# Five edits to the order and size of ScalarE work in a float32 decoder layer

## The chip, the cores and the metric

The kernel runs on one core of one Trainium2 chip. The metric is the device time of one execution in microseconds (us). The core has these engines: TensorE (PE, matrix products), VectorE (DVE), ScalarE (ACT), GpSimd (POOL) and SyncE (SP, which here only starts weight transfers). Each engine works through its own queue of instructions in order; an instruction that has to wait holds up all that stand behind it on the same engine.

## The reference

One decoder layer with 256 tokens, 2048 channels, all in float32:

```python
h = rmsnorm(x, attn_norm_w)
z, xbc, dt_raw, q, k, v, g = split(h @ w_in)
y_ssm  = ssd_mixer(z, xbc, dt_raw, ...) @ w_ssm_out     # 8 groups of 8 heads of 64
y_attn = moba_attention(q, k, v, ...) @ w_attn_out      # 16 heads of 128
g_ssm, g_attn = split(sigmoid(g + b_gate))
x = x + (g_ssm * y_ssm + g_attn * y_attn) @ w_out
h = rmsnorm(x, ffn_norm_w)
u_gate, u_up = split(causal_dwconv(h @ w_up, ...))
x = x + (silu(u_gate) * u_up) @ w_down
```

Inside `ssd_mixer`, the columns `xbc` pass a causal convolution of four taps and silu; silu is also taken of `z`, which multiplies the mixer's result; each group is then normed by its root mean square. With 256 tokens there is one chunk and one attention block, so attention is plain causal attention with a bias by distance, after a norm of each head's query and key.

## The kernel before

**Products.** TensorE takes float32 data in a rounded form, so each operand is split into a high part (a rounded copy) and a low part (the rest), and a product is high x high + high x low + low x high. A weight is fetched in units of 128 x 2048 (1 MB, tile `wraw`, three buffers, started by SP). `unit` (L188) splits each unit in two chunks of 1024 columns: ACT copies the high part (`whi`, L198), DVE subtracts for the low part (`wlo`, L199), three buffers of each. `cm_chunk` (L227) then issues, for each k of a chunk, one matmul of 512 columns with the high part (L234), and afterwards one of 256 columns with the low part (L240). Where the accumulator is only 256 wide, the first becomes two (L237, L238). `last_hi` remembers the high part traced last, and `after_hi()` (L218) puts what is traced in its block behind that high part on ACT's queue: an order of issue, no wait.

**Order.** The Python code is traced once; a scheduler then orders each engine's queue. It issues what is ready first, and among ready instructions the one traced earlier. In the attention stage PE's order alone is fixed as traced. `issue_after(ins)` adds an edge of order.

**The steps of the work, in the order of the trace:**

- Values (L433): column blocks of 512, four units each (`tm_units`, L410; matmuls L401, L402, L407). While block 0 runs, x arrives. After block 1's first unit, `x_squares` (L339) squares x on ACT in four parts of 1024 columns and adds them on DVE (L343 to L345). After the first chunk of that block's third unit, `x_stats` (L347) sums over channels on PE (L350, L312) and forms the norms.
- Attention (`attn_pair`, L469), eight pairs of heads, four units each. What follows the units of a pair is cut into steps that a `Spread` runs one per unit ("tick"): sums of squares at tick 1, the norm at tick 3 (`norm`, L502, with multiplies on GpSimd, L517, for six of the eight pairs), the split of keys and queries at tick 5 (`split`, L519: ACT copies L523, DVE and GpSimd subtract, L525), scores at tick 6. Ahead of pair 6 stands the fourth value column.
- Gates of attention and the attention output.
- The mixer, nine steps. In step g, `group_units` (L779) makes the group's 10 units: four of z (into `pr[:, 0:4]`), then six that pass the convolution (into `pr[:, 4:10]`). Beside them run `core_steps` of the group before: `silu` (L801), transposes, decays (`dec`, L847, with Exp, L860), products (`ydot`, L870), the group's norm (L893 to L905, with Ln and Exp, L329 and L330). `silu` is one activation over all ten parts and is followed by an early load of the ACT table set that holds both Ln and Exp (L804). In steps 1 and 2 four units of the mixer's gates are made each and stored to DRAM (`gs`); in step 8 the other eight stay in `pre[0]`. Steps 3 to 8 also run units of the output product (`out_unit`, L924).
- The last quarter of the output product (L993): eight units, each followed by `merge` (L973). It multiplies the mixer's result by its gate, adds the stored attention part (`ma`) and splits the sum into `mt` (L990, L991). For units 0 to 3 the gate is fetched from `gs` on GpSimd's queue (L977), and two sigmoids follow (L980, L981): of that gate and of a pair of those in `pre[0]`. Both are held behind the last group's norm.
- `out_products` (L1006): the product with `w_out`. The first two units are run together: chunk 0 of both, then chunk 1 of both. x is fetched again for it from ACT's queue (L1002).
- The FFN: up, gate, down, in three thirds.

Of the kernel before, what the change touches and what calls it, by code (L numbers as in the profile page):

```python
# [8 lines left out]
F32 = mybir.dt.float32  # L9
F32R = mybir.dt.float32r  # L10
AF = mybir.ActivationFunctionType
ALU = mybir.AluOpType
AX = mybir.AxisListType
MUL, ADD, SUB, MAX, MIN = ALU.mult, ALU.add, ALU.subtract, ALU.max, ALU.min

DM, T, DI, G, NS, H, HD, DFF = 2048, 256, 4096, 8, 128, 16, 128, 5632
# [109 lines left out]
def mix(x):  # L126
    return x.rearrange("p (a b) -> p b a", a=2)


def mixed(ps):  # L130
    return ps.rearrange("p (b a) -> p b a", a=2)
# [40 lines left out]
def build(nc, d, out):  # L172
    with tile.TileContext(nc) as tc:
        _body(tc, nc, d, out)


def _body(tc, nc, d, out):
    V, S, PE = nc.vector, nc.scalar, nc.tensor
# [39 lines left out]
    def after_hi():  # L218
        return tc.issue_after(last_hi[0].ins) if last_hi[0] is not None else contextlib.nullcontext()

    def mm_tile():
        return psum.tile([128, 512], F32, name="mm", bufs=4)
# [4 lines left out]
    def cm_chunk(ps, part, x2, k0, nk, first, last):  # L227
        hi, lo = part
        wide = ps.shape[-1] == 2 * T
        for k in range(nk):  # L230
            w = hi[:, k * 128:(k + 1) * 128]
            start = first and k == 0
            if wide:
                PE.matmul(ps.rearrange("p (h b a) -> p h b a", h=2, a=2), w,  # L234
                          x2[:, :, k0 + k].rearrange("p h (a b) -> p h b a", a=2), start=start, stop=False)
            else:
                PE.matmul(mixed(ps), w, mix(x2[:, 0, k0 + k]), start=start, stop=False)  # L237
                PE.matmul(mixed(ps), w, mix(x2[:, 1, k0 + k]), start=False, stop=False)  # L238
        for k in range(nk):
            PE.matmul(mixed(ps[:, :T]), lo[:, k * 128:(k + 1) * 128], mix(x2[:, 0, k0 + k]), start=False,  # L240
                      stop=last and k == nk - 1)
# [23 lines left out]
    def r32(name):  # L265
        t = base.tile([128, 2, 16, T], F32R, name=name, tag="s32", bufs=3)
        return t, t[:, 0], t[:, 1]
# [4 lines left out]
    sq = xt_full[:, 16 * T:].rearrange("p (k t) -> p k t", t=T)  # L272
# [44 lines left out]
    def hp_split(k):  # L317
        x = xt[:, k] if k else x0[:, KT:KT + T]
        a = S.activation(hph[:, k], x, AF.Copy, scale=aw[:, k:k + 1])
        return a, V.scalar_tensor_tensor(hpl[:, k], x, aw[:, k:k + 1], hph[:, k].bitcast(F32), op0=MUL, op1=SUB)  # L320

    last_rsq = [None]
# [13 lines left out]
    rb = base.tile([128, T], F32, name="rb")  # L336
    base.tile([128, 16], F32, name="pad1")

    def x_squares():  # L339
        for c in range(4):  # L340
            S.activation(sq[:, 4 * c:4 * c + 4], xt[:, 4 * c:4 * c + 4], AF.Square)
        for c in range(1, 4):
            V.tensor_tensor(sq[:, 0:4], sq[:, 0:4], sq[:, 4 * c:4 * c + 4], op=ADD)  # L343
        V.tensor_tensor(sq[:, 0:2], sq[:, 0:2], sq[:, 2:4], op=ADD)
        V.tensor_tensor(sq[:, 0], sq[:, 0], sq[:, 1], op=ADD)  # L345

# [22 lines left out]
    def bias_rows():  # L369
        rel = ap.tile([REL_BUCKETS + 1, H], F32, name="rel")  # L370
        oh = ap.tile([REL_BUCKETS + 1, 384], F32, name="oh")
        nc.sync.dma_start(rel, d["rel"])
        nc.sync.dma_start(oh, d["onehot"])
        ap.tile([128, 16], F32, name="pad4c")
        ohr = ap.tile([REL_BUCKETS + 1, 384], F32R, name="ohr")
        rels = ap.tile([REL_BUCKETS + 1, 2, H], F32R, name="rels")
        V.tensor_copy(ohr, oh)
        S.activation(rels[:, 0], rel, AF.Copy)
        V.tensor_tensor(rels[:, 1], rel, rels[:, 0].bitcast(F32), op=SUB)
        pb = c_tile()  # L380
        PE.matmul(pb[:H, :384], rels[:, 0], ohr, start=True, stop=False)
        PE.matmul(pb[:H, :384], rels[:, 1], ohr, start=False, stop=True)
        rows = ap.tile([H, 384], F32, name="brows")
        V.tensor_copy(rows, pb[:H, :384])
        nc.gpsimd.dma_start(brow, rows)

    def qk_constants():
        V.tensor_scalar(kscale, sm("kn"), HD ** 0.5, None, op0=MUL)
        same = ap.tile([128, 32], F32, name="same")
        V.tensor_reduce(same, ident.rearrange("p (b i) -> p i b", i=32), axis=AX.X, op=ADD)  # L390
        V.tensor_copy(sel, same[:, None, :].to_broadcast([128, 4, 32]))
# [41 lines left out]
    for cb in range(3):  # L433
        def before(k):
            if k == 0:
                nc.sync.dma_start(xt[:, 1:3], d["xT"][:, 1:3])
            elif k % 2 == 1 and k < 15:
                nc.sync.dma_start(xt[:, k + 2:min(k + 4, 16)], d["xT"][:, k + 2:min(k + 4, 16)])
            elif k == 15:
                nc.sync.dma_start(xt[:, 0:1], d["xT"][:, 0:1])  # L440
            return hp_split(k)

        def after(u, cb=cb):
            if cb == 1 and u == 0:
                with after_hi():
                    x_squares()
            if cb == 1 and u == 2:
                nc.sync.dma_start(small, d["small"])
            if cb == 0 and u == 3:
                bias_rows()  # L450
            if cb == 2 and u == 0:
                qk_constants()
        pst = tm_units(d["wv"][cb], after, before if cb == 0 else None, (lambda: x_stats(ap)) if cb == 1 else None)
        if cb == 0:
            evac0 = pst
            continue
        if cb == 1:
            evac(0, evac0)
        evac(cb, pst)
# [9 lines left out]
    def attn_pair(j):  # L469
# [49 lines left out]
        def split():  # L519
            for key in "kq":  # L520
                n = st["n" + key]
                t = ap.tile([128, 2, 2, T], F32R, name=key + "hl", bufs=1)
                S.activation(t[:, 0], n, AF.Copy)  # L523
                E = V if key == "k" or j in (0, 7) else nc.gpsimd
                E.tensor_tensor(t[:, 1], n, t[:, 0].bitcast(F32), op=SUB)  # L525
                st[key] = t
# [99 lines left out]
    gs = [dram.tile([128, 2, T], F32, name=f"gs{i}") for i in range(KT // 4)]  # L626
# [27 lines left out]
    gate_pool = base  # L654
# [39 lines left out]
    for o in range(KT):  # L694
# [8 lines left out]
        g = gl.pop(o)  # L703
        t = xb.tile([128, T], F32, name="wat", bufs=2)
# [11 lines left out]
    sd = ssd.enter_context(tc.tile_pool(name="ssd", bufs=1))  # L716
# [6 lines left out]
    o = (KT + 10) * T  # L723
# [72 lines left out]
    def core_steps(g):  # L796
        pr = pre[g % 2]
# [1 line left out]
        steps = []  # L799

        def silu():  # L801
            last = S.activation(pr, pr, AF.Silu)
            with tc.issue_after(last.ins):
                S.preload_act_table_set(LN_EXP)  # L804
            bh = sd.tile([128, 2, T + 16], F32R, name="bch")[:, :, :T]
            bl = sd.tile([128, 2, T + 16], F32R, name="bcl")[:, :, :T]
            S.activation(bh, pr[:, 8:10], AF.Copy)
            V.tensor_tensor(bl, pr[:, 8:10], bh.bitcast(F32), op=SUB)
            st["b"] = (bh, bl)

            st["x"] = sd.tile([128, 2, 4, 4, 64], F32R, name="xx")
# [158 lines left out]

    mt2, mh_, ml_ = r32("mt")

    def merge(u, ps):  # L973
        os_ = slice(2 * u, 2 * u + 2)
        if u < 4:
            g = gate_pool.tile([128, 2, T], F32, name="g", bufs=3)
            nc.gpsimd.dma_start(g, gs[u])  # L977
            late = pre[0][:, 2 * u:2 * u + 2]
            with tc.issue_after(last_rsq[0].ins):
                S.activation(g, g, AF.Sigmoid)  # L980
                S.activation(late, late, AF.Sigmoid)  # L981
        else:
            g = pre[0][:, 2 * u - 8:2 * u - 6]
        a = gate_pool.tile([128, 2, T], F32, name="g", bufs=3)
        nc.gpsimd.dma_start(a, ma[u])
        y4 = yacc[:, os_].rearrange("p o (a b) -> p o a b", a=2)
        V.tensor_tensor(y4, ps, y4, op=ADD)
        V.tensor_tensor(yacc[:, os_], yacc[:, os_], g, op=MUL)
        V.tensor_tensor(a, yacc[:, os_], a, op=ADD)
        S.activation(mh_[:, os_], a, AF.Copy)  # L990
        V.tensor_tensor(ml_[:, os_], a, mh_[:, os_].bitcast(F32), op=SUB)  # L991
# [14 lines left out]
    def out_products():  # L1006
        parts = [unit(d["wout"][o]) for o in range(2)]
        pss = [mm_tile() for _ in range(2)]
        for c in range(2):
            for o in range(2):  # L1010
                cm_chunk(pss[o], parts[o][c], mt2, 8 * c, 8, c == 0, c == 1)
        for o in range(KT):
            yield o, pss[o] if o < 2 else cm_unit(d["wout"][o], mt2)

# [4 lines left out]
    for o, ps in out_products():  # L1019
# [6 lines left out]
        else:  # L1026
            t = fp.tile([128, T], F32, name="sqx", bufs=2)
# [91 lines left out]
```

## Time and profile before

| | |
|---|---|
| median of 3 runs | 1955.76 us (1955.42 to 1956.25) |
| the profiled execution | 1955.65 us |
| its span in the profile | 1953.9 us |
| PE busy | 1943.7 us, 99% |
| DVE busy | 1576.6 us, 81% |
| ACT busy | 1253.3 us, 64% |
| GpSimd busy | 78.5 us, 4% |
| granted TensorE clock | 1.00 |
| moved by DMA | 401.81 MB, mean 206 GB/s |

The span is the time from the first to the last instruction that the profiler recorded; the execution's own time is 1.75 us longer. Instructions are named by the line of the kernel that issued them, as "L198 ACT", with the tiles that they write and read. Work of a helper has the helper's line. A row of the timeline gives start, length, engine, line, operation, tiles, shape, count, and in brackets how long the engine had stood idle and who ended it. A row of windows gives the stretch, its width, and then each engine's busy time with its number of instructions: PE, weight loads (PEld), DVE, ACT, POOL; then the granted clock and the DMA's share and rate.

### The profile page before, as it was taken

What the parts mean: (1) busy time and instruction counts of PE and PEld (TensorE: products, weight loads), DVE (VectorE), ACT (ScalarE), POOL (GpSimd) and SP (SyncE); (2) the same over time, 40 slices, a digit from 0 to 9 for tenths busy, and PEclk for the clock granted to TensorE, in tenths of its full rate; (3) what the DMA queues carried; (4) which work ended last, traced back from release to release, by engine and by line L of the source; (5) the groups of instructions that cost most, each with busy time, mean ns of one, the idle gap of its engine ahead of it and who ended that gap; (6) DMA issues with size and microseconds to landing.
All of it is one profiled execution on the core that took longest, in us unless ns stands there. A gap on an engine that the chain in (4) does not pass through costs nothing.

```text
span 1953.9 us, 31462 instructions
## 1 busy us (share of the span) xinstructions
PE 1943.7 (99%) x12287; PEld 1791.6 (92%) x12287; DVE 1576.6 (81%) x2461; ACT 1253.3 (64%) x1894; POOL 78.5 (4%) x100
## 2 busy tenths in 40 slices
PE   9999999999999999999999999999999999999999
PEld 7899899999989999999999998999999999999998
DVE  7588878867789898898989977788888885788665
ACT  6567666545778778777777745566666654566433
POOL 0012210000000000000000000000000000000000
PEclk9999999999999999999999999999999999999999
DMA  8555555766556656555565676555555555555555
GB/s 300 196 198 173 180 192 200 259 210 219 189 192 236 216 183 215 200 208 187 201 217 185 211 267 213 197 207 200 195 206 202 195 206 203 195 204 205 194 191 175
DMA packets 64317, 401.81 MB, mean 206 GB/s; under 512 B 7655, under 2 KB 10264, under 8 KB 20648
## 3 DMA queue, kind: packets, MB, share of 16 engines
q1 hardware_dynamic: 55384, 376.56, 54.6%
q0 software_dynamic: 5760, 18.97, 3.2%
q10 hardware_dynamic: 3024, 4.27, 0.7%
q8 instruction: 96, 1.57, 0.3%
q14 instruction: 53, 0.43, 0.1%
HBM read 394.44 MB, written 5.33 MB: 205 GB/s over the span
## 4 chain that ended last, share of the span: by engine, by line
PE 91%; DVE 3%; ACT 3%; issue 2%; DMA 1%; POOL 1%; DVEq 0%; ACTq 0%; POOLq 0%
PE mm L234 51%; PE mm L240 29%; PE mm L237 3%; PE mm L238 3%; DVE wlo L199 2%; ACT whi L198 1%; PE mm L407 1%; PE mm L401 1%; PE mm L402 1%; PE cc L880 1%; POOL nq L517 0%; PE cc L881 0%; DMA wraw<-wv 0%; PE cc L829 0%; DMA g<-gs 0%
## 5 line engine op out<-in xcount | busy, mean ns | idle before, releaser
L198 ACT ACTIVATE whi<-wraw 128x1024 fp32r<-128x1024 f32 (+1 forms) x712 | 742.3, 1046 | 491.1 <-PE mm L234 349.1
L199 DVE TENSOR_TENSOR wlo<-wraw,whi 128x1024 fp32r<-128x1024 f32 (+1 forms) x712 | 862.2, 1217 | 231.7 <-ACT whi L198 227.6
L234 PE MATMUL mm<-hn,whi 128*128 128x512 f32 x1536 | 363.6, 380 | 1.0 <-ACT whi L198 1.0
L234 PE MATMUL mm<-fh,whi 128*128 128x512 f32 x1408 | 333.3, 379 | 0.1
L234 PEld LDWEIGHTS mm<-hn,whi 128*128 128x128 f32 x1536 | 276.1, 190 | 32.9 <-ACT whi L198 1.2
L234 PEld LDWEIGHTS mm<-fh,whi 128*128 128x128 f32 x1408 | 253.1, 190 | 28.7 <-DVE fh L1022 0.5
L240 PEld LDWEIGHTS mm<-hn,wlo 128*128 128x128 f32 x1536 | 201.4, 191 | 10.3
L240 PE MATMUL mm<-hn,wlo 128*128 128x256 f32 x1536 | 202.4, 275 | 0.0
L240 PEld LDWEIGHTS mm<-fh,wlo 128*128 128x128 f32 x1408 | 184.5, 191 | 9.4
L240 PE MATMUL mm<-fh,wlo 128*128 128x256 f32 x1408 | 185.5, 275 | 0.0
L234 PE MATMUL mm<-hp,whi 128*128 128x512 f32 x768 | 183.2, 381 | 0.9 <-ACT whi L198 0.8
L234 PE MATMUL mm<-a,whi 128*128 128x512 f32 x692 | 164.9, 379 | 0.0
L234 PEld LDWEIGHTS mm<-hp,whi 128*128 128x128 f32 x768 | 138.1, 190 | 17.3 <-ACT whi L198 1.7
L234 PEld LDWEIGHTS mm<-a,whi 128*128 128x128 f32 x692 | 123.8, 190 | 13.5
L237 PE MATMUL mm<-yt,whi 128*128 128x256 f32 x512 | 117.8, 275 | 1.1 <-ACT whi L198 1.1
L238 PE MATMUL mm<-yt,whi 128*128 128x256 f32 x512 | 117.7, 275 | 0.0
L240 PEld LDWEIGHTS mm<-hp,wlo 128*128 128x128 f32 x768 | 100.7, 191 | 5.1
L240 PE MATMUL mm<-hp,wlo 128*128 128x256 f32 x768 | 101.2, 275 | 0.0
L237 PEld LDWEIGHTS mm<-yt,whi 128*128 128x128 f32 x512 | 98.3, 192 | 1.6 <-ACT whi L198 1.5
L238 PEld LDWEIGHTS mm<-yt,whi 128*128 128x128 f32 x512 | 98.3, 192 | 0.3
L240 PEld LDWEIGHTS mm<-a,wlo 128*128 128x128 f32 x704 | 93.4, 191 | 5.0
L1017 DVE TENSOR_TENSOR x<-mm,x 128x256 f32<-128x256 f32 x126 | 53.0, 420 | 53.7 <-PE mm L240 53.7
(315 smaller groups left out, 2464.0 us busy)
## 6 DMA issues: line engine op xcount, KB each, us to landing
wraw<-wup SPq DMA_DIRECT2D x88, 1024.0 KB, 4.8
wraw<-wssd SPq DMA_DIRECT2D x80, 1024.0 KB, 4.8
wraw<-wqk SPq DMA_DIRECT2D x32, 1024.0 KB, 4.7
wraw<-wso SPq DMA_DIRECT2D x32, 1024.0 KB, 4.8
wraw<-wd SPq DMA_DIRECT2D x32, 1024.0 KB, 4.8
wraw<-wga SPq DMA_DIRECT2D x16, 1024.0 KB, 5.0
wraw<-wao SPq DMA_DIRECT2D x16, 1024.0 KB, 5.2
wraw<-wgs SPq DMA_DIRECT2D x16, 1024.0 KB, 4.8
```

Of the source, the lines that this page charges most:

```text
L198: last_hi[0] = S.activation(hi[:, :n // 2], raw[:, s], AF.Copy)
L199: V.tensor_tensor(lo[:, :n // 2], raw[:, s], hi[:, :n // 2].bitcast(F32), op=SUB)
L234: PE.matmul(ps.rearrange("p (h b a) -> p h b a", h=2, a=2), w, x2[:, :, k0 + k].rearrange("p h (a b) -> p h b a", a=2), start=start, stop= ...
L237: PE.matmul(mixed(ps), w, mix(x2[:, 0, k0 + k]), start=start, stop=False)
L238: PE.matmul(mixed(ps), w, mix(x2[:, 1, k0 + k]), start=False, stop=False)
L240: PE.matmul(mixed(ps[:, :T]), lo[:, k * 128:(k + 1) * 128], mix(x2[:, 0, k0 + k]), start=False, stop=last and k == nk - 1)
L401: PE.matmul(mixed(pst[tt]), hph[:, k0 + k, ts], mix(wh), start=first and k == 0, stop=False)
L402: PE.matmul(mixed(pst[tt]), hpl[:, k0 + k, ts], mix(wh), start=False, stop=False)
L407: PE.matmul(mixed(pst[tt]), hph[:, k0 + k, ts], mix(wl), start=False, stop=last and k == 1)
L880: PE.matmul(pt, x0, mt[:, 0:256], start=True, stop=False)
L1017: V.tensor_tensor(halves(x), unmix(ps[:, h * T:(h + 1) * T]), halves(x), op=ADD)
```

## The change

- `x_squares` takes a part: squares 0 and 1 (and one add) after block 1's first unit, squares 2 and 3 (and the other adds) after its second, each behind that unit's high parts.
- The ACT copy of keys and queries in `split` is put behind the high part traced last.
- `silu` becomes two activations: first the six convolved parts, then the four of z. The early table load stays behind the second.
- The four stored gates get one tile, `early`, in the place of tile `xx` of the mixer, and are fetched by four transfers ahead of all merges. The sigmoids are put behind the high part traced last, no longer behind the norm.
- The first two units of `out_products` run k 0 to 7, 8 to 13, 14 and 15, each for both units.

```diff
-    def x_squares():
-        for c in range(4):
+    def x_squares(part):
+        cs = range(2 * part, 2 * part + 2)
+        for c in cs:
             S.activation(sq[:, 4 * c:4 * c + 4], xt[:, 4 * c:4 * c + 4], AF.Square)
-        for c in range(1, 4):
-            V.tensor_tensor(sq[:, 0:4], sq[:, 0:4], sq[:, 4 * c:4 * c + 4], op=ADD)
+        for c in cs:
+            if c:
+                V.tensor_tensor(sq[:, 0:4], sq[:, 0:4], sq[:, 4 * c:4 * c + 4], op=ADD)
+        if part == 0:
+            return
...
-            if cb == 1 and u == 0:
+            if cb == 1 and u < 2:
                 with after_hi():
-                    x_squares()
+                    x_squares(u)
...
-                S.activation(t[:, 0], n, AF.Copy)
+                with after_hi():
+                    S.activation(t[:, 0], n, AF.Copy)
...
         def silu():
-            last = S.activation(pr, pr, AF.Silu)
+            S.activation(pr[:, 4:10], pr[:, 4:10], AF.Silu)
+            last = S.activation(pr[:, 0:4], pr[:, 0:4], AF.Silu)
             with tc.issue_after(last.ins):
                 S.preload_act_table_set(LN_EXP)
...
+    early = sd.tile([128, 4, 2, T], F32, name="early", tag="xx")
+    for u in range(4):
+        nc.gpsimd.dma_start(early[:, u], gs[u])
+
     def merge(u, ps):
...
         if u < 4:
-            g = gate_pool.tile([128, 2, T], F32, name="g", bufs=3)
-            nc.gpsimd.dma_start(g, gs[u])
+            g = early[:, u]
             late = pre[0][:, 2 * u:2 * u + 2]
-            with tc.issue_after(last_rsq[0].ins):
+            with after_hi():
                 S.activation(g, g, AF.Sigmoid)
                 S.activation(late, late, AF.Sigmoid)
...
-        for c in range(2):
+        for k0, nk in ((0, 8), (8, 6), (14, 2)):
             for o in range(2):
-                cm_chunk(pss[o], parts[o][c], mt2, 8 * c, 8, c == 0, c == 1)
+                part = [p[:, k0 % 8 * 128:] for p in parts[o][k0 // 8]]
+                cm_chunk(pss[o], part, mt2, k0, nk, k0 == 0, k0 == 14)
```

## The prediction

> **What bounds the kernel now.** I read the page first: busy time by engine.
>
> ```profile
> span 1953.9 us, 31462 instructions
> PE 1943.7 (99%) x12287; PEld 1791.6 (92%) x12287; DVE 1576.6 (81%) x2461; ACT 1253.3 (64%) x1894; POOL 78.5 (4%) x100
> ```
>
> TensorE (PE) is busy all but 10.2 us. The change removes no matmul, so it can only win PE's idle moments, or make new ones. The view of waits, for PE alone, has two large rows:
>
> ```profile
> PE mm L234 <- ACT whi L198: 1.9, 2, 1.0
> PE mm L237 <- ACT whi L198: 1.1, 2, 0.8
> ```
>
> PE waits above all for a weight's high part (L198), late on ScalarE (ACT). I then cut the span at all places where PE stands (width, then PE busy; the difference is idle):
>
> ```profile
> 34.00:37.00 3.00, 2.38 (x12) 1.77 (x11) 3.00 (x4) 1.06 (x1) 0.00 (x0) 1.00 0.52 202
> 211.00:213.00 2.00, 1.18 (x6) 0.71 (x5) 0.81 (x1) 2.00 (x4) 1.25 (x1) 1.00 0.01 4
> 522.50:524.50 2.00, 1.66 (x14) 1.38 (x13) 1.49 (x3) 2.00 (x5) 0.00 (x0) 1.00 0.00 0
> 579.00:581.00 2.00, 0.97 (x8) 0.75 (x7) 1.73 (x4) 1.98 (x4) 0.00 (x0) 1.00 0.93 381
> 1147.00:1148.50 1.50, 1.22 (x11) 1.03 (x10) 0.77 (x1) 1.50 (x3) 0.00 (x0) 1.00 0.00 0
> 1155.00:1157.50 2.50, 1.66 (x15) 1.47 (x14) 1.57 (x3) 2.50 (x4) 0.54 (x1) 1.00 0.81 301
> 1179.00:1181.00 2.00, 1.39 (x7) 0.88 (x7) 2.00 (x3) 1.49 (x2) 0.00 (x0) 1.00 0.20 82
> ```
>
> Last, the chain of waits (start, length, engine and line), from which later parts draw too:
>
> ```profile
> 521.05 1.28 ACT L804
> ...
> 526.33 0.89 PE mm L240 x8
> 527.22 1.73 PE mm L234 x8
> ...
> 575.00 1.28 ACT L802
> 576.30 2.34 ACT pre L802
> ...
> 580.65 1.99 PE mm L234 x8
> ```
>
> Eight matmuls take 1.73 us in the flow and 1.99 behind a late high part. So a stall costs its idle time and 0.26 us: 0.88 at 34, 1.08 at 211, 0.60 at 522, 1.29 at 579, 0.54 at 1147, 1.10 at 1155, 0.87 at 1179.
>
> **The squares, halved.** On ACT, VectorE (DVE) and PE:
>
> ```profile
> 25.68 3.89 ACT L341 ACTIVATE xt<-xt 128x1024 f32<-128x1024 f32 x4
> 30.54 3.87 DVE L343 TENSOR_TENSOR xt<-xt 128x1024 f32<-128x1024 f32 x3
> 34.32 1.22 DVE L199 TENSOR_TENSOR wlo<-wraw,whi 128x1024 fp32r<-128x1024 f32 x1
> 37.19 0.41 DVE L345 TENSOR_TENSOR xt<-xt 128x256 f32<-128x256 f32 x1
> 41.74 0.50 PE L350 MATMUL cc<-ones,xt 128*128 128x1 f32 x4
> ```
>
> Three adds hold DVE, and the low part at 34.32 is what PE waits for. After: one add (3.87 / 3 = 1.29 us) stands ahead of it, and it is done 2.6 us sooner. Two squares (two times 0.97 us, on ACT), two adds and the short sums (L344, L345) follow one unit later; with the same work in all on DVE, and one low part more ahead of them, L345 ends near 37.6 + 1.2 = 38.8. PE reaches L350 at 41.74 - 0.88 = 40.9: 2.1 us of cover, in which the sum's split (ACT, then DVE) still has to pass. If that is gone, PE waits up to 0.5. Value: -0.88 (bounds -0.9 and 0).
>
> **The split of keys and queries: nothing.** I counted the high parts (L198) issued before the split of pair 4, which stalls PE at 211, and before that of pair 5:
>
> ```profile
> 0.00:208.05 208.05, 67.75 (x65) 1.00 0.62 215
> 0.00:230.72 230.72, 74.96 (x72) 1.00 0.61 211
> ```
>
> The split of a pair is traced at its fifth tick, so behind the next pair's last unit; for pair 4 that is pair 5. High parts up to there: 16 for two value columns and 6 pairs of 8, so the new edge names number 64, and 65 stand ahead already. For pair 5 (its fifth tick ends the fourth value column, 8 more) it names 72, and 72 stand ahead. The edge asks for an order that is there; the splits still wait for GpSimd (POOL), and the next high part still stands behind them. Value: 0 (bounds 0 and -2.2, if the split at 211 and the like one near 233 did move).
>
> **silu in two.** ACT takes 2.34 us for 2560 columns (chain, above) and 1.06 for 1024 (L198, next rows), so 0.83 ns a column and 0.2 us: 1536 columns take 1.49, the 1024 of z 1.06. Where does z go? It is ready after a group's fourth unit, and the scheduler issues what is ready: x's loads (L1002), written behind the last merge, stand 56 us ahead of that merge's last copy (L990).
>
> ```profile
> 1122.50 0.34 ACTq L1002 DMA_DIRECT2D x<-xT  x1
> ...
> 1125.17 1.06 ACT L198 ACTIVATE whi<-wraw 128x1024 fp32r<-128x1024 f32 x1 [0.57 <-PE mm L238]
> ...
> 1146.12 0.63 ACT L980 ACTIVATE g<-g 128x512 f32<-128x512 f32 x1 [6.44 <-DMA g<-gs]
> ...
> 1178.91 0.63 ACT L990 ACTIVATE mt<-g 128x512 fp32r<-128x512 f32 x1 [2.25 <-DVE g L989]
> ```
>
> So I take z's silu, and the preload tied to it, to run far ahead, in ACT's first idle moment. Then the block at 575, with the late high part behind it, is 0.85 shorter (-0.85 of the 1.29). In the first group the preload at 521.05 goes too, bch comes 0.85 + 1.28 sooner, and the stall at 522 goes (-0.60).
>
> The price: the preload no longer stands behind the later silu. A group had two table loads; now it has one for z, the preload, one for the rest, and those that Exp and Ln ask for. Asked for singly, as in the last norm, these two load one each:
>
> ```profile
> 1267.04 1.28 ACT L329 ACT_TABLE_LOAD   x1
> ...
> 1268.76 1.28 ACT L330 ACT_TABLE_LOAD   x1
> ```
>
> So 5 or 6 in place of 2 (Exp, Ln, Exp where a decay's Exp comes first), +3.85 to +5.1 us of ACT in each of 7 groups. A group in the middle:
>
> ```profile
> 852.43 0.84 ACT L860 ACTIVATE m<-m 128x768 f32<-128x768 f32 x1
> ...
> 862.49 0.60 ACT L789 ACTIVATE pre<-g,small 128x256 f32<-128x256 f32 x1 [2.13 <-DVE g L786]
> ...
> 901.57 0.41 ACT L329 ACTIVATE nw<-nw 128x256 f32<-128x256 f32 x1
> ```
>
> and ACT over two groups (its busy time is the fourth):
>
> ```profile
> 640.00:800.00 160.00, 160.00 (x1046) 148.85 (x1045) 142.26 (x216) 127.19 (x191) 5.39 (x10) 1.00 0.60 210
> ```
>
> The decays' last Exp runs at 852, before ACT's idle moments, so z's pair falls into time like the 2.13 us before 862. Around 901 two or three loads delay a high part by 2.6 to 3.8 us, after 2.1 saved (0.85 and the preload). Cover: three buffers of high parts let ACT run two chunks of 2.62 (1.73 + 0.89) ahead of PE; at 575 to 580 ACT issued none for 4.6 us, and 1.29 were lost, so up to some 3.3 us nothing is. Of the 32.8 us that ACT idles in two groups the loads take 8 to 10. Value +0.4 in all (bounds 0 and +4); where the cover is gone, each late microsecond is one of PE's.
>
> By the Trainium skill ("ScalarE: Activation LUTs", Table sets: the hidden batching unit), functions should be done set by set, as each switch costs a load and a drain, about 2.66 us. The trace shows the load alone: from 575.00 silu starts at 576.30. By the page the same switches would cost 8 to 11 us a group, an estimate, and would not fit the cover.
>
> **Gates in one go, sigmoids behind the unit.** The third and fourth gate are fetched when a buffer comes free; ACT stands 6.44 us before the third's sigmoid (above), high parts queued behind it. The fetch, and the last reader of the tile that the new one replaces:
>
> ```profile
> 1139.29 0.54 POOL L977 DMA_DIRECT2D g<-gs  x1 [1.69 <-DVE mt L991]
> 1101.52 0.27 PE L881 MATMUL cc<-mhl,xx 128*128 128x256 f32 x1
> ```
>
> After, the four fetches can go at 1101.8. With 4 x 0.54 us of issue and landing in under 6.4 (1139.83 to 1146.12) they are there by 1110, before the first sigmoid's new place behind the high part of 1125.17. On POOL's queue only the fetches of `ma` stand behind them, 2.2 us later. At 1126 a table load (moved, not added) and 1.26 us of sigmoids fit between two high parts; each later pair adds 1.26 us to a unit of two chunks (5.2). Queued behind a sigmoid are high parts; with nothing in flight none waits. Value -0.54 - 1.10 = -1.64 (bounds -1.7 and, as in the third rival, +0.4).
>
> **First output units in smaller parts.** The stall at 1179 is for the last rows of mt:
>
> ```profile
> 1180.67 0.70 PE L234 MATMUL mm<-mt,whi 128*128 128x512 f32 x2 [0.61 <-DVE mt L991]
> ```
>
> Six steps of k for the other unit (1.73 / 8 + 0.89 / 8 = 0.33 us each, 2.0) and the first's own six low parts (0.7) now come before these, and mt itself comes sooner without ACT's stands. Value -0.87. High and low parts of the first unit are held up to 2 us longer; the one buffer in three that frees as before takes the next unit's: nothing.
>
> **Sum.** 0.88 + 0.85 + 0.60 + 1.64 + 0.87 = 4.84, less 0.4 for the tables: -4.4. The profiled execution took 1955.65 us (span 1953.9 and 1.75 around it), 0.11 below the median of 1955.76. So 1955.65 - 4.4 = 1951.25, and against the median 1951.4.
>
> **Rivals.** *Slower:* z's hoisted half scatters the table sets, and where a high part comes over 3.3 us late PE pays. If half of the 3.85 us in 7 groups lands on PE, that is +13.5: 1965. For it: the loads fall around 901, where high parts, Exp and Ln stand close. Against: the idle time elsewhere, and 2.1 us saved just before. *silu brings nothing:* z runs right behind the other half; the block grows by 0.2, both its gains go, the tables' price too: -3.2, 1952.6. Against: x's loads far ahead. *The fetch stands in the way:* its tile keeps the pool open longer, x's four loads on ACT's queue wait for the fourth gate's product, and high parts stand behind them twice as at 1155: +2.0, 1953.4. For it: x takes that pool's space. Against: it may take another part of it. *The key edge bites:* -2.0 more, 1949.4; the count speaks against it.
>
> **How the numbers follow.** Forecast 55% (its own range 1950.3 to 1952.6), silu nothing 20%, slower 10%, key edge 8%, fetch 7%. Under 0.2% (3.9 us: faster means below 1951.85) this kernel's change can't be told from none. Faster: 0.42 of the forecast, 0.08 key edge, 0.01 else: 0.51. Slower: 0.09, from the table sets above 1959.7 (1.2 us lost a group). Same: 0.40. The range reaches to the other cases but not to 1965: 1949.6 to 1955.6.
>
> **What would show it.** Right: PE not idle at 34, 579, 1147, 1155 and 1179; idle at 211 still, with the same count of high parts ahead; some 40 table loads at silu, Exp and Ln of the groups in place of 16; z's silu 20 us or more before the other. Wrong: z right behind it; PE waiting for L198 in each group near its Ln; ACT waiting at x's loads; a split of keys behind a later high part.

## The result, and the profile after

The changed kernel takes 1971.8 us (median of 6 runs, 1970.57 to 1972.87), the kernel before 1955.18 us beside it (6 runs): ratio 1.0085, 95% interval 1.0072 to 1.0098. It is slower by 0.85%. The forecast was 1951.4 us, a little faster; what came is the rival that had been given one chance in ten, the scattered table sets, and it cost more than the 1965 us put on it.

The page of the changed kernel: span, busy time by engine, and the chain that ended last by engine.

```profile
span 1970.5 us, 31489 instructions
PE 1949.1 (99%) x12287; PEld 1792.8 (91%) x12287; DVE 1576.1 (80%) x2461; ACT 1295.2 (66%) x1935; POOL 78.5 (4%) x100
...
PE 80%; DVE 9%; ACT 8%; issue 2%; POOL 1%; DMA 0%; DVEq 0%; ACTq 0%; POOLq 0%
```

DVE's work is what it was; ACT has 41.9 us and 41 instructions more (1894 before). PE, idle for 10.2 us before, is now idle for 21.4. What it waits for (us in total, times, longest):

```profile
PE mm L240 <- DVE wlo L199: 8.5, 13, 2.1
PE mm L234 <- ACT whi L198: 5.3, 6, 1.4
PE mm L237 <- ACT whi L198: 2.1, 3, 0.9
```

The first row is new: the largest wait is for the *low* part, DVE's, and the others for the high part. Where the stalls lie, in stretches (width, PE busy, weight loads, DVE, ACT, GpSimd, clock, DMA), first around the places that the change was to clear, then in the mixer's groups:

```profile
33.00:38.00 5.00, 5.00 (x25) 4.38 (x24) 5.00 (x7) 2.09 (x3) 0.00 (x0) 1.00 0.99 339
...
209.00:213.00 4.00, 3.19 (x15) 2.49 (x14) 2.65 (x4) 3.50 (x6) 1.57 (x2) 1.00 0.01 2
...
1144.00:1152.00 8.00, 8.00 (x74) 8.00 (x73) 7.13 (x8) 6.65 (x9) 0.00 (x0) 1.00 0.70 231
1152.00:1160.00 8.00, 8.00 (x74) 8.00 (x74) 6.24 (x9) 4.86 (x7) 0.54 (x1) 1.00 0.60 187
1160.00:1187.00 27.00, 27.00 (x245) 27.00 (x244) 24.45 (x31) 14.51 (x17) 2.15 (x4) 1.00 0.86 314
...
600.00:1060.00 460.00, 449.11 (x3005) 416.03 (x3004) 398.83 (x608) 377.76 (x551) 13.45 (x25) 1.00 0.56 198
```

At 34 us and in the whole stretch from 1144 to 1187 PE no longer stands; at 211 it stands as before. But over the mixer's groups, where PE stood not at all before (its row is with the experiments), 10.9 us are idle. The groups of instructions by line show ACT's new work. Before, the table loads of the mixer (L802 is silu, L804 the early load):

```profile
L802 ACT ACT_TABLE_LOAD x8 | 10.3, 1283 | 11.3 <-DVE pre L792 6.5 <-DVE slotA L792 4.8
L804 ACT ACT_TABLE_LOAD x8 | 10.3, 1283 | 0.1
```

After, where silu is L807 (six convolved parts) and L808 (z), the early load L810, the decays' Exp L866, the norm's Ln and Exp L329 and L330:

```profile
L866 ACT ACT_TABLE_LOAD x11 | 14.1, 1283 | 0.2
L329 ACT ACT_TABLE_LOAD x9 | 11.5, 1283 | 0.2
L808 ACT ACT_TABLE_LOAD x8 | 10.3, 1283 | 0.1
L810 ACT ACT_TABLE_LOAD x8 | 10.3, 1283 | 0.1
L807 ACT ACT_TABLE_LOAD x8 | 10.3, 1283 | 11.3 <-DVE pre L797 6.5 <-DVE slotA L797 4.9
L330 ACT ACT_TABLE_LOAD x7 | 9.0, 1283 | 0.1
```

Of L329 and L330 one each is the FFN's norm, as before. So the mixer has 49 loads in place of 16, and 33 x 1.28 = 42 us is all that ACT gained. How such a load becomes time of PE, the chain of waits of the changed kernel shows in one group, step by step (start, length):

```profile
941.16 0.73 ACT m L866
941.89 0.02 issue
941.91 1.28 ACT L808
943.20 0.01 issue
943.21 1.06 ACT slotA L808
944.26 0.27 ACT g L790
944.53 0.48 ACT g L889
...
948.37 0.48 DVE slotA L797
948.86 0.87 DVE mhl L872
949.72 1.15 DVE wlo L199
950.87 0.04 issue
950.91 1.16 PE mm L240 x8
```

Behind the decay's last Exp come the load and the silu of z, and then copies that DVE waits for. DVE's convolution and split end late, the low part stands behind them in DVE's queue, and PE waits for it. From 941 to 951 the chain has no pause longer than 0.04 us. PE's own rows there show the two waits, one for a high part and one for the low part at the chain's end:

```profile
947.99 2.00 PE L234 MATMUL mm<-hn,whi 128*128 128x512 f32 x8 [1.38 <-ACT whi L198]
950.91 1.16 PE L240 MATMUL mm<-hn,wlo 128*128 128x256 f32 x8 [0.93 <-DVE wlo L199]
```

### The profile page after: what moved, and what is told of

Read it like the earlier page. It is cut to its first block, busy times and chain, and to the rows that moved or that the text cites. A ratio compares the mean times of both kernels' runs of the same rounds, so it can differ in the third digit from the quotient of the medians.

```text
span 1970.5 us, 31489 instructions
## 1 busy us (share of the span) xinstructions
PE 1949.1 (99%) x12287; PEld 1792.8 (91%) x12287; DVE 1576.1 (80%) x2461; ACT 1295.2 (66%) x1935; POOL 78.5 (4%) x100
## 4 chain that ended last, share of the span: by engine, by line
PE 80%; DVE 9%; ACT 8%; issue 2%; POOL 1%; DMA 0%; DVEq 0%; ACTq 0%; POOLq 0%
PE mm L234 45%; PE mm L240 25%; DVE wlo L199 3%; ACT whi L198 2%; PE mm L237 2%; PE mm L238 2%; PE mm L405 1%; PE mm L411 1%; PE mm L406 1%; DVE pre L797 1%; DVE slotA L894 1%; ACT m L863 1%; DVE slotA L797 0%; ACT m L864 0%; POOL nq L521 0%
## 5 line engine op out<-in xcount | busy, mean ns | idle before, releaser
L234 PE MATMUL mm<-hn,whi 128*128 128x512 f32 x1536 | 364.3, 380 | 4.5 <-ACT whi L198 4.5
L234 PE MATMUL mm<-fh,whi 128*128 128x512 f32 x1408 | 333.3, 379 | 0.1
L234 PEld LDWEIGHTS mm<-hn,whi 128*128 128x128 f32 x1536 | 276.5, 190 | 37.2 <-ACT whi L198 5.4
L234 PEld LDWEIGHTS mm<-fh,whi 128*128 128x128 f32 x1408 | 253.1, 190 | 28.8 <-DVE fh L1032 0.5
L234 PE MATMUL mm<-hp,whi 128*128 128x512 f32 x768 | 183.2, 381 | 0.9 <-ACT whi L198 0.8
L234 PE MATMUL mm<-a,whi 128*128 128x512 f32 x692 | 164.9, 379 | 0.0
L234 PEld LDWEIGHTS mm<-hp,whi 128*128 128x128 f32 x768 | 138.1, 190 | 17.2 <-ACT whi L198 1.7
L234 PEld LDWEIGHTS mm<-a,whi 128*128 128x128 f32 x692 | 123.8, 190 | 13.5
```

## The experiments

Three theories stood against each other at first; the expectations of the first four runs use their numbers. *1, the tables:* z's silu, issued ahead with the early load tied to it, turns 16 loads into 49, and these make PE wait. *2, z's own activation:* a second activation, and the order of queues that it shifts, costs the time, and not the loads. *3, the other edits:* one of them (sigmoids behind a unit, the fetch in the place of `xx`, smaller output parts) costs the time. A part of the first theory, that a load is free where ACT has idle time and dear elsewhere, was tested after.

**All but silu.** The change, with silu in one piece again:

```diff
-            S.activation(pr[:, 4:10], pr[:, 4:10], AF.Silu)
-            last = S.activation(pr[:, 0:4], pr[:, 0:4], AF.Silu)
+            last = S.activation(pr, pr, AF.Silu)
```

> The changed kernel with silu in one piece again. If silu's split is the whole loss (theories 1 and 2 below), the stalls at the squares, the gates and the first output units are gone (0.88 + 1.64 + 0.87 = 3.4 us) and nothing is added: about 1951.8 against 1955.2 before. If the gates' fetch, the sigmoids or the output units' parts carry the loss (theory 3), it stays near 1971.

Measured: 1952.45 us (1951.9 to 1953.22), ratio to before 0.9987 [0.9978, 0.9996], 23 table loads in all as before. The groups, as a stretch of this kernel:

```profile
600.00:1060.00 460.00, 460.00 (x3139) 431.72 (x3138) 410.10 (x621) 361.47 (x536) 13.49 (x25) 1.00 0.59 203
```

PE does not stand there at all. The other edits do not cost the time; all of the loss is silu's.

**silu alone.** The kernel before, with only this edit:

```diff
-            last = S.activation(pr, pr, AF.Silu)
+            S.activation(pr[:, 4:10], pr[:, 4:10], AF.Silu)
+            last = S.activation(pr[:, 0:4], pr[:, 0:4], AF.Silu)
```

> The kernel before with nothing but silu's split. Theories 1 and 2: the loss of 16.6 us and the 3.4 us that the other edits bring, so +20, about 1975. Theory 3: -1 to 0, about 1954 to 1955.

Measured: 1975.5 us, ratio 1.0105 [1.009, 1.0121], 20.2 us over the 1955.32 us of before beside it, with 56 loads in all in place of 23. The loss is there whole, without the other edits.

**z copied.** The change, with z's silu replaced by a copy and the early load tied to the convolved half. This leaves silu of z out of the computation; the copy needs no set of its own, so its place costs no loads:

```diff
-            S.activation(pr[:, 4:10], pr[:, 4:10], AF.Silu)
-            last = S.activation(pr[:, 0:4], pr[:, 0:4], AF.Silu)
+            last = S.activation(pr[:, 4:10], pr[:, 4:10], AF.Silu)
+            S.activation(pr[:, 0:4], pr[:, 0:4], AF.Copy)
```

> The changed kernel in which z's activation is a copy (so silu of z is left out of the computation) and the early table load is tied to the other half; the copy is as long as silu's (1.06 us) and can be issued as early, but needs no table. It is built with 23 table loads, as the kernel before, where the changed kernel has 56. Theory 1 (the table loads are the cause): the loss is gone, 1950.4 to 1952. Theory 2 (z's 1.06 us of ACT, and the order of queues that it shifts, are the cause): most of the loss stays, 1965 to 1971.

Measured: 1951.71 us, ratio 0.9983 [0.9974, 0.9992], 23 loads. The copy is issued as far ahead (35 us before the convolved half) and takes as long (1.04 to 1.06 us) as z's silu, and costs nothing, as it needs no table. So the loads are the cause, not z's instruction.

**z behind.** The change, with an edge that puts z's silu behind the convolved half:

```diff
-            S.activation(pr[:, 4:10], pr[:, 4:10], AF.Silu)
-            last = S.activation(pr[:, 0:4], pr[:, 0:4], AF.Silu)
+            first = S.activation(pr[:, 4:10], pr[:, 4:10], AF.Silu)
+            with tc.issue_after(first.ins):
+                last = S.activation(pr[:, 0:4], pr[:, 0:4], AF.Silu)
```

> The changed kernel with z's silu pinned behind the other half by one more edge of order, the early load behind both: built with 23 table loads. Theory 1 (the loads are the cause, and the loss is the scattering): the loss is gone, 1951.5 to 1953, near the 1952.45 of the kernel with silu in one piece; the bch stall at 522 stays, since ACT's block before it is as long as before. Theory 2 (any second silu activation costs): 1957 or more.

Measured: 1951.7 us (1951.35 to 1953.03), ratio 0.9982 [0.9973, 0.9991], 23 loads. The same edit with one edge of order more is 20 us shorter than the changed kernel, and beats the kernel before too. Its silu at 575 us, on ACT and then on PE:

```profile
575.27 1.28 ACT L807 ACT_TABLE_LOAD   x1 [1.64 <-DVE pre L797]
576.56 1.48 ACT L807 ACTIVATE pre<-pre 128x1536 f32<-128x1536 f32 x1
...
578.97 1.99 ACT L198 ACTIVATE whi<-wraw 128x1024 fp32r<-128x1024 f32 x2
...
580.06 1.99 PE L234 MATMUL mm<-hn,whi 128*128 128x512 f32 x8 [0.18 <-ACT whi L198]
```

1536 columns take 1.48 us in place of 2.34, and of the stall of 1.03 us here 0.18 is left. z's half stands two high parts further back (581.17), and PE waits for none behind it up to 590.

**The early load late.** The change, with the early load tied to the convolved half and z left free to run ahead:

```diff
-            S.activation(pr[:, 4:10], pr[:, 4:10], AF.Silu)
-            last = S.activation(pr[:, 0:4], pr[:, 0:4], AF.Silu)
+            last = S.activation(pr[:, 4:10], pr[:, 4:10], AF.Silu)
+            S.activation(pr[:, 0:4], pr[:, 0:4], AF.Silu)
```

> The changed kernel, z's silu as free to run ahead as there, but with the early load tied to the other half, which is the later one on the chip: built with 35 loads in place of 56. Theory 1, at 0.4 to 0.6 us a load over 23 (12.7 / 32 measured in the kernel before with loads added, 20 / 33 with silu's split alone): 12 loads are +5 to +7 on the 1951.7 of the kernel with z copied, so 1956.5 to 1959. If instead z's own load in the decays' stretch carries most of it: 1965 or more.

Measured: 1954.7 us, ratio 0.9996 [0.9987, 1.0005], 35 loads, 12 more than before; 3.0 us more than with z behind, beside which it ran. That is 0.25 us for each of the 12, less than expected. (With z copied, which differs only in the copy and so lacks these loads, the kernel was 3.6 us below the one before beside it; this one is 0.3 below.) Ln and Exp of the norm ask for none here; 21 of the 33 loads hung on where the early load stands, and with these 21 went 17 of the 20 us.

**Loads added.** The kernel before, with 32 loads more: one of the set that is in place anyway, behind each Exp of the decays.

```diff
-                S.activation(m, m, AF.Exp, scale=-1.0)
+                ex = S.activation(m, m, AF.Exp, scale=-1.0)
+                with tc.issue_after(ex.ins):
+                    S.preload_act_table_set(LN_EXP)
```

> The kernel before, with one more load of the table set it already holds behind each decay's Exp: 4 in each of 8 groups, 55 loads in all in place of 23, nothing else. Theory 1: 32 loads of 1.283 us, 41 us of ACT, most of it in ACT's dense stretch: +10 to +20, 1965 to 1975. Theory 2: the loads fit ACT's idle time, within 2 us of before.

Measured: 1968.03 us, ratio 1.0065 [1.0053, 1.0078]; 12.7 us over before, 0.40 for each load.

```profile
L862 ACT ACT_TABLE_LOAD x32 | 41.1, 1283 | 0.6
```

A load of a set that is already there takes its full 1283 ns. Loads alone, with silu in one piece, make nearly two thirds of the loss.

**Loads apart.** To find out whether ACT's idle time hides a load, 32 loads were put in the stretch of a group where ACT idles most, behind the convolution's first activation of units 5 to 8:

```diff
-                S.activation(acc, u, AF.Identity, scale=sm("conv_w", 4 * ti + 3), bias=sm("conv_b", ti))
+                ci = S.activation(acc, u, AF.Identity, scale=sm("conv_w", 4 * ti + 3), bias=sm("conv_b", ti))
+                if 5 <= i < 9:
+                    with tc.issue_after(ci.ins):
+                        S.preload_act_table_set(LN_EXP)
```

> The kernel before with the same 32 added table loads as in the run with loads added (55 in all), but each behind the first tap of a convolved unit (units 5 to 8 of a group), where ACT idles 1 to 2 us a unit. If a load costs only where it makes a high part later than the cover of some 3.3 us: 0 to +4, 1955 to 1959. If each load costs a flat 0.4 us wherever it stands: +12.7, 1968.

Measured: 1967.17 us, ratio 1.006 [1.0047, 1.0072], 12.2 us over before: the same 0.4 per load. Of each load's 1.28 us some 0.9 are hidden, but ACT's idle time hid no more than the dense stretch behind the decays' Exp did. Why, ACT and then DVE show:

```profile
642.22 1.28 ACT L792 ACT_TABLE_LOAD   x1
643.52 2.00 ACT L198 ACTIVATE whi<-wraw 128x1024 fp32r<-128x1024 f32 x2
```

```profile
644.61 2.36 DVE L199 TENSOR_TENSOR wlo<-wraw,whi 128x1024 fp32r<-128x1024 f32 x2 [0.66 <-ACT whi L198]
```

```profile
656.39 1.28 ACT L805 ACT_TABLE_LOAD   x1 [1.68 <-DVE slotA L795]
```

The high part is late behind the load, so the low part is, DVE stands 0.66 us, and the convolution's steps behind it in DVE's queue are late. ACT then still waits its 1.68 us for the convolution's last step at silu (1.60 before): this idle time was not room, it was the other half of one chain through both engines.

From 660 us on PE does not pay at the loads, but once in each group, behind the next silu, and in the kernel with loads added it pays at the same places. One of them, with loads added and then with loads apart:

```profile
662.48 1.99 PE L234 MATMUL mm<-hn,whi 128*128 128x512 f32 x8 [1.63 <-ACT whi L198]
```

```profile
662.04 1.99 PE L234 MATMUL mm<-hn,whi 128*128 128x512 f32 x8 [1.82 <-ACT whi L198]
```

Neither wait is in the kernel before. The next five lie at 742, 822, 902, 981 and 1061 us in both kernels, 0.9 to 1.7 us each. The last load of the group stands 29 us ahead of silu's own load with loads added (627.99 and 656.83) and 8 us with loads apart (647.96 and 656.39). So the four loads of a group, 5.1 us, add up, and ACT does not win back between them and silu what they cost. How far ahead ACT is shows in its waits for PE to free a buffer of high parts: from 600 to 1060 us there are 21 at the matmuls L234 before, 13 with loads apart and none with loads added.

At this point two readings were left: every load costs 0.4 us wherever it stands, or it costs where ACT and DVE run as one chain with little to spare, and cannot get ahead of PE again.

**Loads in the FFN** tell these apart: 31 loads more, of the set that silu needs, in the FFN, where ACT feeds a DVE with time to spare:

```diff
-                S.activation(c, u, AF.Identity, scale=sm("fconv_w", 3 * ti + 2), bias=sm("fconv_b", ti))
+                cf = S.activation(c, u, AF.Identity, scale=sm("fconv_w", 3 * ti + 2), bias=sm("fconv_b", ti))
+                if half and th < 2:
+                    with tc.issue_after(cf.ins):
+                        S.preload_act_table_set("silu_and_others")
```

> Before with 31 more table loads of the set that silu needs anyway (54 in place of 23), each behind a convolution activation of the feed-forward's second half tile, where ACT sits idle some 1 us in front of each whi and whi is made some 2 us ahead of the matmul that reads it. If a load costs only through a late high part (ACT and DVE without room in a mixer group): under 1 us for all 31. If a load costs a flat 0.4 us wherever it stands, as in the two runs with 32 loads in the groups: 12 us more than before, 1967.

Measured: 1954.7 us beside 1954.9 for before, ratio 0.9999 [0.999, 1.0008]: 31 loads, 40 us more of ACT, and no time that shows (by the interval at most 1.6 us, where a flat price gives 12).

```profile
L1065 ACT ACT_TABLE_LOAD x32 | 41.1, 1283 | 0.6
```

```profile
1502.69 1.28 ACT L1065 ACT_TABLE_LOAD   x1
1503.98 1.06 ACT L198 ACTIVATE whi<-wraw 128x1024 fp32r<-128x1024 f32 x1
...
1506.42 1.06 ACT L198 ACTIVATE whi<-wraw 128x1024 fp32r<-128x1024 f32 x1 [0.81 <-PE mm L234]
```

```profile
1400.00:1600.00 200.00, 200.00 (x1222) 183.59 (x1221) 170.65 (x269) 147.67 (x211) 0.00 (x0) 1.00 0.57 201
```

The high part behind the load comes late, and the next one already waits for a free buffer again (0.81 us, released by PE): the lead is back within one unit. Over 200 us, with 19 of the loads in them, PE never stands. In the kernel before, without loads, the same stretch and the groups read:

```profile
1400.00:1600.00 200.00, 200.00 (x1223) 183.68 (x1223) 170.64 (x269) 123.98 (x192) 0.00 (x0) 1.00 0.57 201
600.00:1060.00 460.00, 460.00 (x3138) 431.72 (x3137) 409.80 (x621) 361.25 (x536) 13.45 (x25) 1.00 0.58 203
```

So there is no flat price; the place sets it. DVE's share is close, 85% in the FFN and 89% in the groups; ACT's is 62% and 79%. What ends ACT's idle time differs more: in the FFN it waits for PE to free a buffer for 56.0 of 200 us, in the groups for 16.7 of 460 (both at L234) and otherwise mostly for DVE. Which of the two decides, that ACT has more room or that DVE does not hold it up, no run separates.

**The three other terms, each alone** in the kernel before: the squares in two parts; gates and sigmoids; the first output units in three parts (each with its hunk of the change's diff and nothing else).

> Of the change only the squares of x in two parts. The prediction's term: the stall of PE at 34 us (0.62 idle, 0.88 with its gap) goes, 0.9 us less than before; 23 table loads as before. If what one stall gives back is eaten at the next wait, as silu's block was, no difference from before (within 0.3 us).

> Of the change only the merge: four gates fetched ahead and the sigmoids issued behind a unit's high part. The prediction's term: the two stalls at 1147 and 1155 us go, 1.6 us less than before, the out stage's stall near 1179 (0.77) stays. If PE only comes earlier to the next late high part, the out stage's stall grows and less than 0.6 us is won.

> Of the change only the first output units in three parts (8, 6 and 2 blocks). The prediction's term: the stall near 1179 us goes, 0.9 us less than before; the stalls at 1147 and 1155 stay. If the last part of mt only comes as late as before, the stall moves from the second half to the last two blocks, and nothing is won.

Measured, beside 1954.9 us for before: squares 1954.12 us, ratio 0.9996 [0.9987, 1.0005]; merge 1952.7, ratio 0.999 [0.9981, 0.9999]; output 1953.87, ratio 0.9996 [0.9987, 1.0005]. Only the second is clear of no change by its interval; the medians stand 0.8, 2.2 and 1.0 us below before. The stretches 1143 to 1160 (for the output's kernel from 1150) and 1170 to 1187, of the squares' kernel, the merge's, and the output's:

```profile
1143.00:1160.00 17.00, 17.00 (x153) 16.90 (x152) 12.34 (x16) 9.60 (x12) 2.69 (x5) 1.00 0.59 205
1170.00:1187.00 17.00, 16.39 (x100) 14.47 (x99) 15.05 (x21) 8.91 (x12) 0.00 (x0) 1.00 0.67 241
```

```profile
1143.00:1160.00 17.00, 17.00 (x154) 17.00 (x154) 14.74 (x19) 8.81 (x11) 1.61 (x3) 1.00 0.73 264
1170.00:1187.00 17.00, 17.00 (x110) 15.71 (x109) 13.27 (x19) 9.24 (x12) 0.00 (x0) 1.00 0.56 200
```

```profile
1150.00:1160.00 10.00, 9.53 (x85) 9.34 (x85) 8.02 (x11) 4.20 (x6) 1.61 (x3) 1.00 0.78 286
1170.00:1187.00 17.00, 17.00 (x109) 15.49 (x108) 15.26 (x22) 9.74 (x14) 0.00 (x0) 1.00 0.58 196
```

The merge's edit clears the second stretch too, by itself; the output's clears it as well. So these two share one stall of 0.6 us, and what they measure alone can't be added up. And the squares' kernel, in which the merge is as before, has no stall from 1143 to 1160 in its profiled execution: these two stalls are not in every execution of the old merge.

**Keys one step later.** z behind, with the split of keys and queries moved one tick later, to remove the stalls at 211 and 233 that the change left:

```diff
-                sp.add([[sums("k"), split_sums], [], [norm_sum, norm], [], split], 5, first=True)
+                sp.add([[sums("k"), split_sums], [], [norm_sum, norm], []], 4, first=True)
...
-                steps = [[], [], [], [], [], [scores(0), scores(1), soft(0), soft(1)], [], [ptr(0), ptr(1)], []] + values
+                steps = [[], [], [], [], [], [split, scores(0), scores(1), soft(0), soft(1)], [], [ptr(0), ptr(1)], []] + values
```

> The kernel with z pinned, and the split of keys and queries moved one tick later, just before its scores, so that the edge names the high parts of one more unit. If the splits standing before a high part are what stalls PE at 185, 210 and 232 (0.2 + 1.0 + 1.0, and 0.26 behind each): 2.2 to 2.9 us less than the kernel with z pinned alone, about 1949.5. Rival: the split then comes too late for the scores on PE, which stand in a fixed order; PE waits there instead, no gain or a loss of up to 8 x 1 us.

Measured: 1952.86 us, ratio 0.9988 [0.9979, 0.9997], 1.2 us over z behind: a miss. On PE:

```profile
200.76 1.99 PE L234 MATMUL mm<-hp,whi 128*128 128x512 f32 x8 [1.39 <-ACT whi L198]
```

The stalls at 211 and 233 are gone, and a larger one stands at 200, where on ACT the exponentials of the softmax stand right ahead of the high part; another of 0.98 us stands at 226. The stalls were moved, not removed.

## Why the prediction was wrong

The step that failed is **"silu in two"**, and in it the price of the tables: "Value +0.4 in all (bounds 0 and +4)". The edit alone measured +20.2 us. With the gains of this step taken at 0.4 us (z behind is 3.3 below the kernel before beside it, all but silu 2.9; so only roughly), the tables cost about 20.6. The mechanism had been seen and priced among the rivals. That z runs far ahead, and about how many loads follow, were right; what covers them was not.

- *Where z goes:* right in that it runs far ahead. In the group shown its load runs at 941.91, straight behind the decays' last Exp, 36 us ahead of the other half's at 977.77.
- *How many loads:* "5 or 6 in place of 2" in 7 groups, so 21 to 28 more; there were 33. The decays' Exp asks for 11 of them: six in the first part of a group, behind silu or the norm's Ln, and five where z's silu runs ahead of the last Exp, while the prediction had it behind.
- *"ACT's first idle moment":* wrong. ACT stood 0.1 us in all ahead of the eight loads of z (row L808 above): at 860.67 and 941.91 z went into the dense stretch of the decays' last Exps, ahead of copies that DVE needs. And the idle time of 2.13 us was ACT waiting for DVE's sum in front of the convolution (L786), while DVE waits in turn for ACT's copies and high parts. What makes one of the two late makes the next step of this one chain late. Loads apart shows it, with loads right behind the activation that such a wait holds up.
- *"Up to some 3.3 us nothing is [lost]":* wrong. That cover was worked out from one place, 575 to 580, where a full stock of high parts stood ahead, and for ACT's high parts alone. PE's largest wait is for the low part, 8.5 of 18 us, and no lead of DVE had been reckoned. Each place was also held against the full cover by itself, while the loads of a group add up: two more in most groups cost 3.0 us in all (the early load late), four more 12.2 and 12.7. Near the norm's Ln, where the price was looked for, little is lost; most of the stalls are around z's load and silu and around the next silu, and the largest, 2.06 us, is at 1094.88, beside the last group's decays.
- *The rival's arithmetic:* half of 3.85 us in 7 groups gave +13.5, so 1965. From the second silu's load (575.0 before, 575.5 after) to the eighth, at 1043.8 before and 1059.4 after, six groups take 15.1 us longer, 2.5 in each, where 1.9 was assumed; the rest is lost before and behind these. In all, PE waits 25 times in the changed kernel and 18.0 us, in all but silu 7 times and 5.1 us; 12.9 us more, and 18 stalls more at 0.26 us each (4.7), make 17.6 of the 19.9 us between the two spans.

By the Trainium skill ("ScalarE: Activation LUTs", Table sets: the hidden batching unit) functions are to be done set by set. That rule spoke against this edit, and here the trace agrees: the mixer has 33 loads more, and silu's edit alone cost 20 us. The page's figure for a switch (What ACT_TABLE_LOAD costs), about 2.66 us with a drain, is not what this trace has: a load takes 1.28 us, and silu starts 0.01 us behind it (941.91 and 943.21 in the chain above). No run here shows the drain. What a load cost the program was on average between 0 and about 0.6 us (20 / 33), by its place and by how many stood in one group.

The other steps:

- *silu's shorter block* (-0.85): right in size where z is held behind. PE's idle time at 579 goes from 1.03 to 0.18 us, and the changed kernel has its stall there shortened as well (0.23). *The stall at 522* (-0.60): it goes in the changed kernel and with z copied, but with z behind it stays, as the early load then stands ahead of `bch`. With z copied the stall at 579 is what it was (1.04), so no kernel without the extra loads has both gains.
- *Squares* (-0.88): PE's idle time at 34 is gone; -0.8 by the medians, not clear of nothing by the interval.
- *Keys* (0): right; the stall at 211 is what it was (0.81 us idle of 4 in the row above, 0.82 before). So is the one near 233 (0.79 us, 0.82 before), which the prediction names here but leaves out of its list of places where PE stands.
- *Gates and sigmoids* (-1.64) and *output units* (-0.87): alone -2.2 and -1.0; each of them clears the stall at 1179, so the two measured values don't add up. The gates' term was taken from the stalls of one execution, and the old stalls at 1147 and 1155 come and go; how much of the -2.2 is theirs is open.
- *The fetch in the way:* did not come; PE is busy throughout from 1144 to 1187. *silu brings nothing* did not come, as z ran ahead. Where z is held behind, the kernel is 3.3 us below the one before beside it, close to that rival's 3.2, but not for its reason: high parts are issued between the halves, and the 0.85 of the block is won.
- Without silu's price the sum of the rest was -3.4 (0.88, 1.64, 0.87); all but silu measured -2.9 (1952.45 against 1955.32), which agrees within the interval of some 1.8 us on either side. The three measured alone give 4.0 (0.8, 2.2 and 1.0), more than the 2.9 together, as the gates and the output units clear the same stall.

## What to carry to other kernels

An activation that is cut in two, or freed to run earlier, takes its table set with it: count the loads that the new order asks for, at every reader of the other set, and pin both parts together (one edge of order was worth 20 us here). Before filling idle time on ScalarE, look at what ends it and at who reads the next result: here it was room where ACT waited for PE to free a buffer (the FFN), and cost time where ACT waited for a VectorE that waits for ACT in turn (the mixer). Add up what is put in front of one critical place, also when it stands tens of us ahead. A cover worked out at one stall, for one engine, holds there and not for the engine behind it.

## What the runs showed of the hardware that was not expected

- A load of a set that is in place already takes as long as any: 1283 ns, in 32 of 32 behind the decays' Exp and in the 31 added in the FFN.
- The same load cost 0.40 us of the program's time behind the decays' Exp (12.7 / 32), 0.38 behind the convolution (12.2 / 32), 0.25 where only z ran ahead (3.0 / 12), and nothing in the FFN (31 loads). The first two agree, and their stalls lie in the same places: behind silu, once in each group from 660 us on.
